# Rotary embedding on one core: the second batch's load is issued by SyncE instead of ScalarE

## The chip, the cores and the metric

The kernel runs on one core of a Trainium2 chip. The metric is the device time of one execution in microseconds (us); less is better. Three executions were timed before the change.

## What is computed

The reference rotates pairs of halves of each head (16 heads of 64 numbers) by tables that depend on the position in the sequence alone:

```python
# x: (16, 512, 1024) f32; cos, sin: (512, 32) f32
x = x.reshape(16, 512, 16, 64)
x1, x2 = x[..., :32], x[..., 32:]
out = concatenate([x1 * cos - x2 * sin, x1 * sin + x2 * cos], axis=-1)
```

So 33.55 MB are read, 33.55 MB are written, and three elementwise passes lie between: a product with cos, a product of the swapped halves with plus or minus sin, and a sum.

## The kernel before

**Tiles.** The work is cut into 64 "rows", each a block of 128 partitions x 1024 numbers (half a megabyte). Ten tiles of x hold them. Tiles 0, 1, 8 and 9 are one batch each (4 rows, 2 MB, moved in pieces of 16 KB); tiles 2 to 7 are two batches each (8 rows, 4 MB, moved in pieces of 32 KB). In the list `tiles`, tile 1 is batch 1, "the second batch". Rows are numbered u = 0 to 63 through all tiles, so tile 7 is rows 48 to 55, tile 8 rows 56 to 59 and tile 9 rows 60 to 63.

**Memory.** `x_sb` is a ring of 40 rows: tiles 0 to 5. Tiles 6 to 9 reuse its places, so their loads wait for stores of earlier tiles. Results are written in place, and stored from there.

**Engines.** For each row VectorE (DVE) multiplies x by cos into PSUM (`mul`, line 293). GpSimd (POOL) multiplies the swapped halves by sin into one of six buffers `t2_sb` (line 257); row 3 of each pair tile is done by VectorE instead (line 286). The sum is made in one of two ways: VectorE adds (`comb`, line 304), or, for the 21 rows with u mod 8 in 1, 3, 6 of the pair tiles and of rows 56 to 59, TensorE adds by a product with the identity (line 224) and ScalarE (ACT) copies the sum out of PSUM (line 191). PSUM has three places for rows (`t1_ps`), so `mul` of row u needs row u-3 to be gone.

**Tables.** cos and sin (64 KB each) are loaded into `stage` (line 174). VectorE copies cos for the single tiles (line 264), ScalarE makes the signed sin table (lines 182, 183), and TensorE and ScalarE make the pair tables (lines 208, 186, 187). GpSimd's first row waits for the sin table, VectorE's first row for the cos table.

**Transfers.** All loads are issued by ScalarE, from `load` (line 153), in this order: tile 0, cos, sin, tile 1, tiles 2 to 5. After row 17 ScalarE waits until the stores of tiles 0 and 1 have landed and loads tile 6; after row 25 it waits for the store of tile 2 and loads tile 7; after row 33 it waits for the store of tile 3 and loads tiles 8 and 9. ScalarE works in order, so its copy of the next row (line 191) stands behind that wait. Stores are issued by SyncE (SP), tile by tile (line 161), each when all rows up to the tile's last are summed. The last act is SyncE's wait for the stores (line 162). Loads and stores thus use two DMA queues: q10 for what ScalarE issues, q1 for what SyncE issues.

Of the kernel before, what the change touches and what calls it, by code (L numbers as in the profile page):

```python
# [6 lines left out]
def bass_split_heads_rope_kernel(  # L7
# [60 lines left out]
    with ExitStack() as stack:  # L68
# [44 lines left out]
        def in_dram(single, pairs, t):  # L113
            b, n = tiles[t]
            return single[b] if n == R1 else pairs[:, b:b + 2, :]

        def in_sbuf(t):
            b, n = tiles[t]
            k = b * R1 % RING
            return x_sb[:, k:k + n].rearrange("p n h t d -> p (n h t d)")  # L120

        def where(u):
            t, r = rows[u]
            return t, r, u % RING
# [7 lines left out]
        def wait_added(eng, u):  # L132

            if n_pe[u]:
                eng.wait_ge(sem_a, n_pe[u])
            if n_comb[u]:
                eng.wait_ge(sem_v, n_comb[u])
# [10 lines left out]
        def stores_of(k):  # L148

            return sum(b * R1 // R2 == k for b, _ in tiles)  # L150

        def load(eng, t):
            eng.dma_start(in_sbuf(t), in_dram(x1, x2, t)).then_inc(sem_in[t], 16)  # L153

        def on_sync(sp):
            for u in range(NU):
                t, r, k = where(u)
                if r == tiles[t][1] - 1:
                    wait_added(sp, u)
                    k = u // R2  # L160
                    sp.dma_start(in_dram(o1, o2, t), in_sbuf(t)).then_inc(sem_out[k] if k < EARLY else sem_rest, 16)
            sp.wait_ge(sem_rest, 16 * sum(stores_of(k) for k in range(EARLY, NU // R2)))

        def on_scalar(ae):
            later = {}
            for t, (b, n) in enumerate(tiles):
                if b * R1 + n <= RING:
                    load(ae, t)
                else:

                    later.setdefault((b * R1 - RING) // R2 * R2 + R2 - 1 + LAG, []).append(t)
                if t == 0:
                    for i, (table, sem) in enumerate(((cos, sem_cos), (sin, sem_sin))):
                        ae.dma_start(stage[:, i, :], table.rearrange("(s r) d -> s (r d)", r=R1)).then_inc(sem, 16)  # L174

            ae.wait_ge(sem_i, 2)
            ae.activation(  # L177
                pick[:], ident[:].rearrange("q (s k) -> q k s", k=2)[:, :, :, None].broadcast_to([P, 2, P // 2, 2]), COPY
            ).then_inc(sem_g, 1)
            ae.wait_ge(sem_sin, 16)  # L180
            sv = stage[:, 1, :].rearrange("s (r d) -> s r d", d=HALF)
            ae.activation(s1_sb[:, :, 0, :], sv, COPY, scale=-1.0)  # L182
            ae.activation(s1_sb[:, :, 1, :], sv, COPY).then_inc(sem_s, 1)  # L183
            ae.wait_ge(sem_t, 2)
            s2 = s2_sb[:].rearrange("p (k r) t d -> p k r t d", r=R1)
            ae.activation(s2[:, :, :, 0, :], pair_ps[:, :, 1, :, :], COPY, scale=-1.0)  # L186
            ae.activation(s2[:, :, :, 1, :], pair_ps[:, :, 1, :, :], COPY).then_inc(sem_s, 1)  # L187
            for u in range(NU):
                if PE2[u]:
                    ae.wait_ge(sem_e, n_pe[u])  # L190
                    ae.activation(xs[:, u % RING, :], t1_ps[:, u % NT1, :], COPY).then_inc(sem_a, 1)  # L191
                for t in later.get(u, ()):
                    k = (tiles[t][0] * R1 - RING) // R2
                    ae.wait_ge(sem_out[k], 16 * stores_of(k))
                    load(ae, t)
# [65 lines left out]
        def on_vector(ve):  # L261
# [49 lines left out]
            for u in range(NU + LEAD):  # L311
                if u < NU:
                    mul(u)
                if u >= LEAD and not PE2[u - LEAD]:
                    comb(u - LEAD)

        on_sync(nc.sync)
        on_scalar(nc.scalar)
        on_gpsimd(nc.gpsimd)
        on_tensor(nc.tensor)  # L320
# [34 lines left out]
```

## Time and profile before

| What | us |
| --- | --- |
| median of the three timed runs (161.17 to 161.33) | 161.23 |
| span of the profiled execution, first to last instruction | 160.3 |

The page gives no time of the profiled execution but its span; the 0.9 us by which the median is longer lie around the first and last instruction, and are taken as the same for any version. Below, 0 is the first instruction.

Busy in that span: GpSimd 134.9 us (84%), VectorE 130.3 us (81%), TensorE 72.8 us, ScalarE 24.4 us. The DMA engines moved 67.26 MB at a mean of 419 GB/s, and 0.99 of 16 engines' span is the two queues' share (49.6% and 48.9%).

The trace gives each transfer's issue and the time from issue to landing:

| Tile | load issued | load landed | store issued | store landed |
| --- | --- | --- | --- | --- |
| 0 | 0.81 | 8.8 | 20.48 | 39.1 |
| cos / sin | 1.21 / 1.69 | 9.0 / 9.2 | | |
| 1 | 2.17 | 14.1 | 31.02 | 53.6 |
| 2 | 2.87 | 23.8 | 47.50 | 73.6 |
| 3 | 3.47 | 38.4 | 63.68 | 93.06 |
| 4 | 4.13 | 52.9 | 81.07 | 112.1 |
| 5 | 4.79 | 72.3 | 102.73 | 126.7 |
| 6 | 53.60 | 91.9 | 119.57 | 141.2 |
| 7 | 73.60 | 111.3 | 135.58 | 150.7 |
| 8 | 93.08 | 126.5 | 143.57 | 155.5 |
| 9 | 93.45 | 141.0 | 151.70 | 160.3 |

A row of the profile's timeline reads: start, duration, engine, line, operation, output<-input, count of merged instructions, and in brackets the idle time before and what ended it. "ACTq" and "SPq" are the queues that ScalarE and SyncE issue transfers from; their rows are the issue, not the transfer.

### The profile page before, as it was taken

What the parts mean: (1) busy time and instruction counts of PE and PEld (TensorE: products, weight loads), DVE (VectorE), ACT (ScalarE), POOL (GpSimd) and SP (SyncE); (2) the same over time, 40 slices, a digit from 0 to 9 for tenths busy, and PEclk for the clock granted to TensorE, in tenths of its full rate; (3) what the DMA queues carried; (4) which work ended last, traced back from release to release, by engine and by line L of the source; (5) the groups of instructions that cost most, each with busy time, mean ns of one, the idle gap of its engine ahead of it and who ended that gap; (6) DMA issues with size and microseconds to landing.
All of it is one profiled execution on the core that took longest, in us unless ns stands there. A gap on an engine that the chain in (4) does not pass through costs nothing.

```text
span 160.3 us, 522 instructions
## 1 busy us (share of the span) xinstructions
PE 72.8 (45%) x94; PEld 24.0 (15%) x94; DVE 130.3 (81%) x117; ACT 24.4 (15%) x27; POOL 134.9 (84%) x64
## 2 busy tenths in 40 slices
PE   6050004478357936660847105489458435850000
PEld 1020002022202211210221002022202111220000
DVE  0069998599989999996999709899889999999500
ACT  0420000203120222022012010201220402040000
POOL 1059999999999999999999999699999999289400
PEclk9955555557755587689687965555555977699555
DMA  5999999999999999999999999999999999999896
GB/s 147 409 441 474 409 450 409 425 429 429 446 429 458 417 411 466 409 433 401 450 433 425 425 409 458 409 433 433 411 429 462 441 417 401 450 441 441 376 450 294
DMA packets 3170, 67.26 MB, mean 419 GB/s; under 512 B 352, under 2 KB 608, under 8 KB 608
## 3 DMA queue, kind: packets, MB, share of 16 engines
q10 hardware_dynamic: 1728, 33.69, 49.6%
q1 hardware_dynamic: 1440, 33.56, 48.9%
q14 instruction: 2, 0.02, 0.0%
HBM read 33.69 MB, written 33.55 MB: 419 GB/s over the span
## 4 chain that ended last, share of the span: by engine, by line
DMA 60%; POOL 13%; DVE 8%; PE 7%; issue 3%; ACT 2%; ACTq 1%; DVEq 0%
DMA x_sb<-in_x_dram 41%; DMA out_dram<-x_sb 18%; POOL t_sb L257 13%; PE t_ps L224 7%; DVE t_ps L293 5%; DVE x_sb L304 3%; ACT x_sb L191 2%; ACTq L153 1%; ACTq L174 1%; DVE t_sb L286 0%; DVEq L303 0%
## 5 line engine op out<-in xcount | busy, mean ns | idle before, releaser
L257 POOL TENSOR_TENSOR t_sb<-x_sb,s_sb 128x1024 f32<-128x1024 f32 x58 | 134.2, 2346 | 14.8 <-ACT s_sb L183 8.5
L224 PE MATMUL t_ps<-t_sb,ident 128*128 128x512 f32 x84 | 68.0, 957 | 63.0 <-DVE t_ps L293 39.2
L293 DVE TENSOR_TENSOR t_ps<-x_sb,pair_ps 128x1024 f32<-128x1024 f32 x48 | 57.7, 1223 | 9.9 <-ACT x_sb L191 9.8
L304 DVE TENSOR_TENSOR x_sb<-t_ps,t_sb 128x1024 f32<-128x1024 f32 x43 | 52.4, 1218 | 2.6 <-POOL t_sb L257 2.6
L224 PEld LDWEIGHTS t_ps<-t_sb,ident 128*128 128x128 f32 x84 | 22.1, 290 | 108.9 <-DVE t_ps L293 74.6
L191 ACT ACTIVATE x_sb<-t_ps 128x1024 f32<-128x1024 f32 x21 | 21.5, 1023 | 109.9 <-PE t_ps L224 96.9
L293 DVE TENSOR_TENSOR t_ps<-x_sb,tab_ps 128x1024 f32<-128x1024 f32 x16 | 19.3, 1222 | 0.1
L286 DVE TENSOR_TENSOR t_sb<-x_sb,tab_ps 128x1024 f32<-128x1024 f32 x6 | 7.3, 1213 | 0.0
L264 DVE COPY tab_ps<-stage 128x128 f32<-128x128 f32 x1 | 0.3, 294 | 7.8 <-DMA stage<-in_cos_dram 7.8
L208 PE MATMUL pair_ps<-stage,pick 128*128 128x256 f32 x4 | 2.0, 667 | 5.4 <-DMA stage<-in_sin_dram 5.4
L201 PE MATMUL t_ps<-zero 128*128 128x512 bf16 x6 | 2.7, 627 | 1.3 <-DVE zero L262 1.3
L208 PEld LDWEIGHTS pair_ps<-stage,pick 128*128 128x128 f32 x4 | 1.2, 324 | 6.4 <-issue 6.3
L177 ACT ACT_TABLE_LOAD x1 | 1.3, 1283 | 5.5 <-issue 5.5
L201 PEld LDWEIGHTS t_ps<-zero 128*128 128x128 bf16 x6 | 0.7, 136 | 2.4 <-DVE zero L262 1.2
L262 DVE MEMSET zero<- 128x256 uint32 x1 | 0.3, 272 | 0.9 <-PEq L337 0.9
L186 ACT ACTIVATE s_sb<-pair_ps 128x256 f32<-128x256 f32 x1 | 0.4, 383 | 1.7 <-PE pair_ps L208 1.7
L182 ACT ACTIVATE s_sb<-stage 128x128 f32<-128x128 f32 x1 | 0.3, 309 | 2.1 <-DMA stage<-in_sin_dram 2.1
L235 POOL MEMSET ident<- 128x128 f32 x1 | 0.2, 204 | 0.3 <-POOLq L337 0.3
L177 ACT ACTIVATE pick<-ident 128x256 f32<-128x256 f32 x1 | 0.4, 416 | 0.0
L187 ACT ACTIVATE s_sb<-pair_ps 128x256 f32<-128x256 f32 x1 | 0.4, 379 | 0.0
L237 POOL TENSOR_SCALAR_AFFINE_SELECT ident<-ident 128x128 f32<-128x128 f32 x1 | 0.3, 292 | 0.1
L337 POOL MEMSET const-float32-0.0<- 128x1 f32 x1 | 0.1, 98 | 0.3 <-issue 0.3
(6 smaller groups left out, 1.0 us busy)
## 6 DMA issues: line engine op xcount, KB each, us to landing
x_sb<-in_x_dram ACTq DMA_DIRECT2D x6, 4096.0 KB, 38.0
out_dram<-x_sb SPq DMA_DIRECT2D x6, 4096.0 KB, 25.0
x_sb<-in_x_dram ACTq DMA_DIRECT2D x4, 2048.0 KB, 22.6
out_dram<-x_sb SPq DMA_DIRECT2D x4, 2048.0 KB, 15.2
stage<-in_cos_dram ACTq DMA_DIRECT2D x1, 64.0 KB, 7.8
stage<-in_sin_dram ACTq DMA_DIRECT2D x1, 64.0 KB, 7.5
```

What stands on the lines that cost most here:

```text
L153: eng.dma_start(in_sbuf(t), in_dram(x1, x2, t)).then_inc(sem_in[t], 16)
L174: ae.dma_start(stage[:, i, :], table.rearrange("(s r) d -> s (r d)", r=R1)).then_inc(sem, 16)
L177: ae.activation(pick[:], ident[:].rearrange("q (s k) -> q k s", k=2)[:, :, :, None].broadcast_to([P, 2, P // 2, 2]), COPY).then_inc(sem_g, 1)
L186: ae.activation(s2[:, :, :, 0, :], pair_ps[:, :, 1, :, :], COPY, scale=-1.0)
L191: ae.activation(xs[:, u % RING, :], t1_ps[:, u % NT1, :], COPY).then_inc(sem_a, 1)
L201: pe.matmul(t1_ps[:, k, b * BANK:(b + 1) * BANK], zero[:, 0:P], zero[:], start=True, stop=True).then_inc(sem_w, 1)
L208: pe.matmul(pair_ps[:, k].rearrange("p c r d -> p (c r d)"), pick[:, k].rearrange("q s b -> q (s b)"), stage[:].rearrange("q c f -> q (c f)"),
L224: ins = pe.matmul(t1_ps[:, u % NT1, b * BANK:(b + 1) * BANK], ident[:], t2[:, b * BANK:(b + 1) * BANK], start=False, stop=True, skip_group ...
L257: pl.tensor_tensor(t2_sb[:, u % NT2, :, :, :], swapped(k), over_heads(s_of(t, r)), mult).then_inc(sem_p, 1)
L286: ve.tensor_tensor(t2_sb[:, u % NT2, :, :, :], swapped(k), over_heads(v_ps), mult)
L293: ve.tensor_tensor(t1_ps[:, u % NT1, :].rearrange("p (h d) -> p h d", d=HALF), x_sb[:, k, :, :, :].rearrange("p h t d -> p (h t) d"), c_of ...
L304: ve.tensor_tensor(xs[:, k, :], t1_ps[:, u % NT1, :], t2_sb[:, u % NT2, :, :, :].rearrange("p h t d -> p (h t d)"), add,).then_inc(sem_v, 1)
```

## The change

SyncE issues the load of tile 1 as its first act, before its first store. ScalarE skips tile 1 in its loop and goes from the sin table straight to tile 2. Buffer, semaphore, size and pieces of the load are the same; what changes is which queue carries it and when it is issued. No wait is added or removed.

```diff
         def on_sync(sp):
+            load(sp, 1)
             for u in range(NU):
                 t, r, k = where(u)
                 if r == tiles[t][1] - 1:
...
             for t, (b, n) in enumerate(tiles):
+                if t == 1:
+                    continue
                 if b * R1 + n <= RING:
                     load(ae, t)
```

## The prediction

> **What bounds the kernel now.** I read the page first, for the share of the DMA engines:
>
> ```profile
> span 160.3 us, 522 instructions
> ...
> DMA  5999999999999999999999999999999999999896
> GB/s 147 409 441 474 409 450 409 425 429 429 446 429 458 417 411 466 409 433 401 450 433 425 425 409 458 409 433 433 411 429 462 441 417 401 450 441 441 376 450 294
> ```
>
> After the first slice the engines that move data never rest. No byte is added or removed, so the end stays where it is as long as some queue always holds work; the question is whether a hole opens. For that I need the start, the sharing between the queues, and the end. The start, from the timeline:
>
> ```profile
> 0.81 0.37 ACTq L153 DMA_DIRECT2D x_sb<-in_x_dram  x1
> ...
> 1.21 0.46 ACTq L174 DMA_DIRECT2D stage<-in_cos_dram  x1
> ...
> 1.69 0.45 ACTq L174 DMA_DIRECT2D stage<-in_sin_dram  x1
> ...
> 2.17 3.27 ACTq L153 DMA_DIRECT2D x_sb<-in_x_dram  x5
> ...
> 9.04 0.29 DVE L264 COPY tab_ps<-stage 128x128 f32<-128x128 f32 x1 [7.84 <-DMA stage<-in_cos_dram]
> 9.26 0.31 ACT L182 ACTIVATE s_sb<-stage 128x128 f32<-128x128 f32 x1 [2.08 <-DMA stage<-in_sin_dram]
> ...
> 9.85 32.35 POOL L257 TENSOR_TENSOR t_sb<-x_sb,s_sb 128x1024 f32<-128x1024 f32 x14 [8.48 <-ACT s_sb L183]
> ```
>
> All computing waits for tile 0, cos and sin, which are alone at the head of the queue and land at 8.8, 9.0 and 9.2; GpSimd starts at 9.85 and pauses little after. How two busy queues share, from the DMA view of two stretches: 26 to 52 us, where stores go in 16 KB pieces against loads in 32 KB pieces,
>
> ```profile
> q10 hardware_dynamic: 251, 7.34, 65.9%
> q1 hardware_dynamic: 254, 3.85, 34.6%
> ```
>
> and 56 to 72 us, where both have 32 KB pieces (columns: packets, MB, share of the engines):
>
> ```profile
> q1 hardware_dynamic: 114, 3.47, 50.9%
> q10 hardware_dynamic: 120, 3.41, 49.3%
> ```
>
> The queues take turns piece by piece: equal counts, bytes by size. The middle, from the timeline at 92 to 98 us:
>
> ```profile
> 93.08 2.40 ACTq L153 DMA_DIRECT2D x_sb<-in_x_dram  x2
> 95.52 1.02 ACT L191 ACTIVATE x_sb<-t_ps 128x1024 f32<-128x1024 f32 x1 [8.86 <-issue]
> 96.58 1.23 DVE L293 TENSOR_TENSOR t_ps<-x_sb,pair_ps 128x1024 f32<-128x1024 f32 x1 [5.31 <-ACT x_sb L191]
> ```
>
> ScalarE stands until tile 3's store lands (93.06), issues two loads in 2.40 us, and only then empties a place of PSUM that VectorE has wanted for 5.31 us. From there VectorE hardly pauses (three gaps of 0.41 us), so its later times hang on that landing. The end:
>
> ```profile
> 135.58 16.46 SPq L161 DMA_DIRECT2D out_dram<-x_sb  x3
> ...
> 141.02 9.27 POOL L257 TENSOR_TENSOR t_sb<-x_sb,s_sb 128x1024 f32<-128x1024 f32 x4 [3.92 <-DMA x_sb<-in_x_dram]
> ...
> 148.10 1.23 DVE L304 TENSOR_TENSOR x_sb<-t_ps,t_sb 128x1024 f32<-128x1024 f32 x1
> 150.40 1.23 DVE L304 TENSOR_TENSOR x_sb<-t_ps,t_sb 128x1024 f32<-128x1024 f32 x1 [1.08 <-POOL t_sb L257]
> ```
>
> The store of tile 7 is issued at 135.58, 5.6 us before tile 6's lands (141.2); tile 9's at 151.70, 3.8 us before tile 8's lands (155.5). These leads keep the engines full at the end. After 141 us there are no loads left to fill a hole.
>
> **Step 1: the issue.** ScalarE loses one issue (about 0.6 us; five take 3.27 us), so tiles 2 to 5 are issued that much earlier, into a queue that is full until they come: worth 0. ScalarE's next work waits for sin anyway. SyncE gains one issue; its next duty is the first store at 20.48, so nothing stands behind it: 0. A rule speaks against a gain: the Trainium skill, "DMA: Bandwidth & Descriptors", section "Issuing engines are not separate DMA queues", says that issuing from several engines saves only the time to issue; taken alone it would leave 161.2 us, while the turns above make it worse than that.
>
> **Step 2: the start.** Tile 0 now shares the engines with tile 1, 16 KB pieces against 16 KB pieces, from the first. Before, 2 MB cost 4.85 us (tile 1 landed 14.05, sin 9.25, 4.80 apart). Tile 0 ends after 15 or 16 turns instead of 8, and cos and sin stand behind it in its queue. The bytes of the four transfers are the same, so sin, now the last of them, lands where tile 1 did: 14.05, a shift of 4.8. If tile 0 leads by a turn, cos and sin end one piece earlier: 4.2 (4.85/8 = 0.6 a piece). With no sharing it would be 0, which the rows above speak against. I take 4.8. GpSimd starts at 14.65, and its fourth row, which makes the first store, shifts alike: 20.48 becomes 25.3.
>
> **Step 3: the middle.** Stores now enter the queue 4.8 us later. Their rate is set by turns against a load queue that is still full, so each lands 4.8 later: tiles 0 and 1 at 58.4, tile 2 at 78.4, tile 3 at 97.9. Loads use the freed turns and run about 4.8 us ahead: tile 5 at 67.5, tile 6 at 87.1, tile 7 at 106.5. Is the load queue ever empty? Tile 6 is issued at 58.4 (before 67.5), tile 7 at 78.4 (before 87.1), tiles 8 and 9 from 97.9 (before 106.5): no. So no hole here, and nothing lost yet. But ScalarE's stand also ends 4.8 later, and VectorE's stall of 5.31 with it: computing gets nothing back. GpSimd's waits for loads (3.92 and 0.38 us) vanish, but VectorE, which trails GpSimd by some 6 us at tile 7 (row 55: GpSimd ends at 127.9, VectorE's sum starts at 134.3), has none of them to gain.
>
> **Step 4: the end.** Tile 7's store is issued at 135.58 + 4.8 = 140.4. Up to 141.2 all other bytes are the same, so tile 6's store still lands at 141.2: the lead shrinks from 5.6 to 0.8. How long a transfer into idle engines takes to start bounds the hole. From below: tile 9's store landed 4.85 after tile 8's, with no start to pay. From above: tile 0's load, alone in a cold queue, took
>
> ```profile
> DMA to landing us min/median/max: 8.0/8.0/8.0
> ```
>
> from issue to landing for the same 2 MB, so 8.0 - 4.85 = 3.15 of start. I take 2.35, nearer to the load, since that row contains its very first pieces. Tile 7 then lands at 140.4 + 2.35 + 9.7 = 152.4 (before 150.7), tile 8 at 157.3, tile 9 at 162.1, if tile 9's store comes in time. It comes so: VectorE's last tile loses its wait of 1.08 on GpSimd, which now has its data early, so its last sum shifts by 4.8 - 1.17 (150.40 would be 149.23 behind the sum that starts at 148.10): issue at 151.70 + 3.63 = 155.3. Alone it lands 4.85 + 2.35 = 7.2 later: 162.5, with the bounds 160.2 and 163.3. The later of the two counts: 162.5 instead of 160.3, that is +2.2, on the median 163.4. A page's price for one transfer (same page, section on the anatomy of one DMA, fitted for GpSimd's transfers: 2.0 us and bytes at 436 GB/s) gives an estimate of 6.8 instead of the row's 8.0, and 163.0 instead of 163.4 for the sum.
>
> The unknowns: the shift (4.2 to 4.8: -0.6), the start (3.15: +0.8; none at all: -2.3, which would leave only the absorbed case below), TensorE's clock, which is granted by turns at 0.5 and 1.0 and makes the three gaps of 0.41 (up to -1.2, or as much more), and the 2.40 us of two issues at 93.08, where two issues at the start take 0.8 (up to -1.6). Not all fall on one side: +0.6 to +3.2.
>
> **The rivals.** *Absorbed, 161.2.* The engines stay full and the bytes alone set the end. It holds if tile 7's store shifts by less than about 3 us (its lead of 5.6 less 2.35) and tile 9's issue by less than about 1.5 (3.8 less 2.35), or two or three of the unknowns fall together: 4.8 - 1.6 - 1.2 = 2.0 at tile 7, 0.8 at tile 9. For it: the DMA row full of nines, GpSimd's 4.3 us of waits for loads. Against it: VectorE, not GpSimd, releases tile 7, and waits for no load. *No sharing, 161.2 or a little less.* SyncE's pieces come only after tile 0, cos and sin; then the start is as before, and perhaps the ramp (the first 4 us carry 147 GB/s) is a little fuller, by at most 0.5 us. The equal piece counts speak against it. *Whole shift, 164.6 to 166.0.* The last tile does not catch up its 1.17, or a stall of ScalarE grows: 156.5 + 7.2 = 163.7 of span for the first, 160.3 + 4.8 for the rest of the shift.
>
> **How the numbers follow.** A hole at the end as summed: 0.77. Whole shift: 0.10. Absorbed: 0.09, a fifth of it with a small loss. No sharing: 0.04, mostly a little faster. A measurement of this kernel can tell about 0.2% (0.3 us) from no change: faster 0.03, same 0.08, slower 0.89. The range 161.8 to 164.6 takes in the first case and the near edge of the third.
>
> **What would show it.** Sin landing near 14 us, GpSimd starting near 14.6 and the first store near 25; the waits for loads on GpSimd gone; tile 3's store landing near 97.9 and VectorE starting again near 101.4; the DMA row with a dent at about 141 to 143 us; last store issued near 155.3. I am wrong if GpSimd starts before 13 us, if tile 7's store is issued before 138.5, or if the DMA row has no dent and the end still moves.

## The result, and the profile after

The changed kernel takes 162.03 us (median of eight, 161.41 to 163.18) where the kernel before takes 161.26 (eight, 161.17 to 161.49): ratio 1.0045, 95% interval 1.0027 to 1.0064, some 0.7 us slower. Forecast were 2.2 us. The mechanism is the one that was summed; its size was three times too large. The profiled execution of the changed kernel has a span of 160.9 us and a time of 162.30, so 1.4 us lie around the span.

The page:

```profile
span 160.9 us, 522 instructions
...
DMA  5999999999999999999999999999999999999997
GB/s 183 424 428 432 497 416 391 391 411 428 452 424 448 399 436 458 448 399 440 464 399 432 473 399 407 497 395 395 456 454 432 440 407 420 391 391 391 428 420 326
...
POOL 32%; DMA 26%; PE 14%; DVE 12%; issue 6%; ACT 4%; ACTq 1%; DVEq 0%
```

The DMA row has no visible dent, which by its letter is one of the prediction's signs of being wrong. But a slice is 4 us, and the hole that opened is 1 us (slices 35 to 37 have 391 GB/s, the whole span 418); the windows at the end of this section show it. The chain of work that ended last (last line) tells more: before, 60% of it was DMA; now DMA has 26%, and the computing engines have most of the rest. The start, from the timeline (the changed kernel's lines are 3 higher than before's, so L267 is L264, L296 is L293, L260 is L257, L194 is L191):

```profile
0.80 0.38 SPq L153 DMA_DIRECT2D x_sb<-in_x_dram  x1
0.81 0.40 ACTq L153 DMA_DIRECT2D x_sb<-in_x_dram  x1
...
13.60 0.29 DVE L267 COPY tab_ps<-stage 128x128 f32<-128x128 f32 x1 [12.40 <-DMA stage<-in_cos_dram]
13.78 0.31 ACT L185 ACTIVATE s_sb<-stage 128x128 f32<-128x128 f32 x1 [7.22 <-DMA stage<-in_sin_dram]
...
14.37 2.35 POOL L260 TENSOR_TENSOR t_sb<-x_sb,s_sb 128x1024 f32<-128x1024 f32 x1 [13.00 <-ACT s_sb L186]
```

Tile 0 lands at 13.4, tile 1 at 13.2, cos at 13.6, sin at 13.8: the four transfers end together, as turns piece by piece make them. GpSimd starts 4.5 us later than before. The middle, at 97 to 101 us:

```profile
98.06 0.86 ACTq L153 DMA_DIRECT2D x_sb<-in_x_dram  x2
98.97 1.02 ACT L194 ACTIVATE x_sb<-t_ps 128x1024 f32<-128x1024 f32 x1 [7.54 <-DMA out_dram<-x_sb]
100.03 1.23 DVE L296 TENSOR_TENSOR t_ps<-x_sb,pair_ps 128x1024 f32<-128x1024 f32 x1 [3.24 <-ACT x_sb L194]
```

Tile 3's store lands at 98.04 (97.9 was forecast), but the two load issues behind it take 0.86 us instead of 2.40, and VectorE goes on at 100.03, not at 101.4. The end, with the time of tile 9's store from issue to landing in the second fence:

```profile
139.36 15.48 SPq L162 DMA_DIRECT2D out_dram<-x_sb  x3
...
152.09 2.35 DVE L307 TENSOR_TENSOR x_sb<-t_ps,t_sb 128x1024 f32<-128x1024 f32 x2
```

```profile
L162 SPq DMA_DIRECT2D out_dram<-x_sb x1: 338/338/338, 154.5 to 154.5; - x1
DMA to landing us min/median/max: 6.3/6.3/6.3
```

VectorE ends without its wait on GpSimd, as forecast. Tile 7's store is issued at 139.36, 1.04 us before tile 6's lands (140.40), and lands at 150.89. That is 10.49 after tile 6's, where a second profile of the kernel before has 9.49: the hole, 1.0 us. Tiles 8 and 9 follow after 4.92 and 5.04 instead of 4.84 and 4.82. The windows from 136 to 144 us show the hole too (the last two columns: share of the DMA engines, GB/s), first the second profile of before, then the changed kernel:

```profile
136.00:144.00 8.00, 5.76 (x8) 1.87 (x6) 6.91 (x7) 2.05 (x2) 4.37 (x3) 0.68 1.03 442
```

```profile
136.00:144.00 8.00, 5.62 (x7) 1.51 (x5) 7.59 (x8) 1.02 (x1) 8.00 (x4) 0.52 0.80 344
```

The packets in the trace give it piece by piece. In the changed kernel the 16 engines are through with tile 6's store between 139.3 and 140.0, up to 1.1 us before its landing is signalled at 140.40, and tile 7's first piece starts at 140.56, 1.20 us after its issue. On average an engine stands idle 1.06 us between 136 and 144 us, and 0.01 us in the second profile of before.

### The profile page after: what moved, and what is told of

Its sections match the earlier page's. It is cut to its first block, busy times and chain, and to the rows that moved or that the text cites. A ratio compares the mean times of both kernels' runs of the same rounds, so it can differ in the third digit from the quotient of the medians.

```text
span 160.9 us, 522 instructions
## 1 busy us (share of the span) xinstructions
PE 73.0 (45%) x94; PEld 23.5 (15%) x94; DVE 130.1 (81%) x117; ACT 24.4 (15%) x27; POOL 134.8 (84%) x64
## 4 chain that ended last, share of the span: by engine, by line
POOL 32%; DMA 26%; PE 14%; DVE 12%; issue 6%; ACT 4%; ACTq 1%; DVEq 0%
POOL t_sb L260 32%; DMA out_dram<-x_sb 19%; PE t_ps L227 14%; DMA stage<-in_sin_dram 7%; DVE t_ps L296 6%; DVE x_sb L307 4%; ACT x_sb L194 4%; ACTq L153 1%; DVE t_sb L289 1%; ACTq L177 0%; ACT s_sb L185 0%; ACT s_sb L186 0%; DVEq L293 0%
## 5 line engine op out<-in xcount | busy, mean ns | idle before, releaser
L260 POOL TENSOR_TENSOR t_sb<-x_sb,s_sb 128x1024 f32<-128x1024 f32 x58 | 134.1, 2356 | 13.7 <-ACT s_sb L186 13.0
L296 DVE TENSOR_TENSOR t_ps<-x_sb,pair_ps 128x1024 f32<-128x1024 f32 x48 | 57.7, 1222 | 8.9 <-ACT x_sb L194 8.9
L194 ACT ACTIVATE x_sb<-t_ps 128x1024 f32<-128x1024 f32 x21 | 21.5, 1024 | 109.0 <-PE t_ps L227 96.9
L227 PEld LDWEIGHTS t_ps<-t_sb,ident 128*128 128x128 f32 x84 | 21.6, 284 | 108.4 <-DVE t_ps L296 68.9
L296 DVE TENSOR_TENSOR t_ps<-x_sb,tab_ps 128x1024 f32<-128x1024 f32 x16 | 19.3, 1222 | 0.6 <-ACT x_sb L194 0.6
L267 DVE COPY tab_ps<-stage 128x128 f32<-128x128 f32 x1 | 0.3, 295 | 12.4 <-DMA stage<-in_cos_dram 12.4
```

The lines of the kernel that those rows point to most:

```text
L227: ins = pe.matmul(t1_ps[:, u % NT1, b * BANK:(b + 1) * BANK], ident[:], t2[:, b * BANK:(b + 1) * BANK], start=False, stop=True, skip_group ...
L260: pl.tensor_tensor(t2_sb[:, u % NT2, :, :, :], swapped(k), over_heads(s_of(t, r)), mult).then_inc(sem_p, 1)
L296: ve.tensor_tensor(t1_ps[:, u % NT1, :].rearrange("p (h d) -> p h d", d=HALF), x_sb[:, k, :, :, :].rearrange("p h t d -> p (h t) d"), c_of ...
```

## The experiments

**The theory**: tile 1's pieces push tile 0 and the tables back; all stores shift with them; ScalarE's wait for tile 3's store passes the shift on to VectorE; tile 7's store comes too late to keep the engines full. **Its rivals**: a second queue of loads is slow by itself; or the loss is in proportion to the delay, wherever it is made. All ratios are against the kernel before on the same chip, with their 95% intervals.

**The changed kernel again, and the same delay on one queue.** No edit in the first. In the second, tile 1 stays on ScalarE, and the tables go behind it:

```diff
-                if t == 0:
+                if t == 1:
                     for i, (table, sem) in enumerate(((cos, sem_cos), (sin, sem_sin))):
```

> The changed kernel once more, as the reference for this group and a second profile of it. Theory 'late start, hole at the end': GpSimd starts at 14.4, the stores of tiles 0 to 3 land 5 us later than before, the DMA row has a dent near 139 to 141 us, and the time is 161.4 to 163.2 us, scattered more widely than before because the end now hangs on VectorE and ScalarE, not on the bytes. Where the second of the two load issues after tile 3's store takes 2.0 us instead of 0.5, the time should be about 1.5 us longer. Rival 'two queues of loads are slower': no dent, and the share of the DMA engines in 8 to 24 us below 1.0.

> All loads on ScalarE's queue as before the change, but cos and sin behind tile 1: one queue, the start late by 4.8 us, nothing on SyncE. Theory 'late start': GpSimd starts at 14.6, tile 7's store is issued 3.3 to 4.8 us later than before (138.9 to 140.4), the hole is there, and the time is 162.0 to 163.2 us. As the ramp of the first 4 us is that of one queue, tile 6's store lands at 141.2, not 140.4, and the time is a little above that of the changed kernel. Rival 'two queues of loads are slower' expects 161.2 us, since there is one queue.

The changed kernel: 161.86 us, ratio 1.0042 (1.0019 to 1.0065), last landing 160.40. One queue: 161.70, 1.0031 (1.0006 to 1.0056), GpSimd starting at 14.63, tile 7's store at 138.63, last landing 160.24. Nothing is issued by SyncE at the start there, and the loss is the same within the intervals: it is the delay that costs. Nor does the changed kernel's second profile show the rival's sign, less busy DMA engines at 8 to 24 us: their share there is 1.04, and 1.01 in the second profile of before. Three numbers of the expectation for one queue failed: it was no slower than the changed kernel, its time lay under the 162.0 forecast, and tile 7's store was issued before 138.9.

**Half the delay**, one queue: the tables behind the first two rows of tile 1, the other two after them. (`half(eng, t, i)` loads share i of two equal shares of tile t's rows. Its definition, and the waits for such a tile, raised from 16 to 32, are not shown here and below.)

```diff
+                if t == 1:
+                    half(ae, 1, 1)      # rows 2 and 3
...
                 if t == 0:
+                    half(ae, 1, 0)      # rows 0 and 1
```

> One queue, half the delay: cos and sin behind the first two rows of tile 1 (all 128 partitions, 8 KB pieces), the other two rows after them. The start is late by 2.4 us (GpSimd at 12.2). Theory 'late start, hole at the end': tile 7's store is issued at 136.5 to 138.0, still early enough; no dent, time as before (161.4 to 161.6 us). A loss in proportion to the delay expects half of what the two late versions lost (0.3 to 0.4%), that is about 161.8 us.

161.42 us, ratio 1.0003 (0.9995 to 1.0012). GpSimd starts at 12.05, 2.4 late; tile 7's store is issued at 135.92, 4.9 us before tile 6's lands. The first 2.4 us cost nothing that can be measured; a loss in proportion, 0.15 to 0.2%, lies just above the interval.

**Twice the delay**, one queue: the tables behind tile 1 and four rows of tile 2.

```diff
+                if t == 2:
+                    half(ae, 2, 1)
...
-                if t == 0:
+                if t == 1:
+                    half(ae, 2, 0)
```

> One queue, about twice the delay: cos and sin behind tile 1 and the first four rows of tile 2, so the start is late by 9.65 us (GpSimd near 19.3). Theory 'late start, hole at the end': once the lead is used up, every further microsecond counts in full. Against the changed kernel (late by 4.5) everything shifts by another 5: tile 7's store issued near 144.2, tile 9's near 159.3, last landing 6.3 us later at 165.5 to 166, against 159.8 to 160.3 before; ratio 1.033 to 1.038. A loss in proportion to the delay, drawn through the changed kernel's 0.4% at 4.5 us, expects 0.9%.

162.91 us, ratio 1.0106 (1.0089 to 1.0122). GpSimd starts at 19.50, but the rest of the theory's numbers failed: I had taken every microsecond beyond the lead to count in full, and 5 us more cost 1. The loss in proportion, 0.9%, came nearest here; what speaks against it is half the delay, and below the later wait, with the whole delay and no loss. What gave way is VectorE's stall, from its waits:

```profile
DVE t_ps L303 <- ACT x_sb L201: 4.9, 9, 1.4
```

(total, times, longest), against 9.5 and 3.2 in the changed kernel. All early loads have landed at 62.63, tile 6's is issued only at 62.84, and its first piece moves at 67.10, 4.3 us later. The DMA view of 62.7 to 67 us has packets of the store queue q1 and none of q10 (the share passes 100% because a packet counts whole where it starts):

```profile
q1 hardware_dynamic: 61, 2.00, 117.4%
```

Meanwhile the stores have all the turns: tile 2's store takes 16.2 us after tile 1's instead of 20, and tile 3's lands at 98.37, no later than in the changed kernel. ScalarE hardly stands. Now GpSimd is the path:

```profile
POOL 71%; DMA 10%; issue 7%; DVE 3%; PE 2%; ACTq 1%; ACT 1%
```

It runs without a pause from 19.50 to 153.53. Holes open all the same at the end: an engine stands idle 0.97 us on average between 136 and 158 us. That the chain passes a delay on in full holds only as long as the load queue has work.

**Finer stores at the end**, in the changed kernel and in the one before: tiles 7, 8 and 9 are stored in two halves of rows each.

```diff
-                if r == tiles[t][1] - 1:
+                n = tiles[t][1]
+                if t in (7, 8, 9) and (r + 1) % (n // 2) == 0:
...
+                    sp.dma_start(d[:, f] if n == R1 else d[:, :, f], in_sbuf(t)[:, f]).then_inc(sem_rest, 16)
+                elif r == n - 1:
```

> The changed kernel with the stores of tiles 7, 8 and 9 issued in two halves of rows each, so that data is at hand earlier at the end. Theory 'late start, hole at the end': the first half of tile 7's store is issued near 131 us, before tile 6's store has landed, so the dent in the DMA row at 138 to 141 goes; the last half tile is issued near 154 and needs about 4 us, so it no longer sets the end; span 159.6 to 160.0, time 161.0 to 161.3 us on a chip where the kernel before takes 161.5, with less scatter. Rival 'the loss is made at the start, by sharing': 161.9 us as without the finer stores.

> The same finer stores in the kernel before, where tile 7's store already waits in the queue. Theory: no hole to close, 161.4 to 161.6 us, the same as before. If finer stores are a gain by themselves (an earlier last landing), it is faster by as much as the changed kernel is with them, some 0.6 us.

Changed kernel: 161.54 us, ratio 1.0016 (1.0006 to 1.0025). Before: 161.36, 1.0003 (0.9994 to 1.0012). The first half of tile 7 is issued at 132.80, no idle time of the DMA engines is left between 136 and 158 us, and the loss falls from 0.42 or 0.45% to 0.16% (the intervals of 0.42 and 0.16 still overlap); where there was no hole, finer stores bring nothing. The rest was larger than I expected, hence the next pair.

**ScalarE's waits three rows later** (all three of them), in both kernels, leaves the late start and takes VectorE's stall away:

```diff
-    LAG = 10
+    LAG = 13
```

> The changed kernel with ScalarE's wait for a store (and the load behind it) three rows later: after rows 20, 28 and 36 instead of 17, 25 and 33. In the changed kernel ScalarE stands until 98.0 us with row 35's sum not copied, and VectorE is idle 3.2 us for it (1.9 at the stand before). If the loss goes through this stand, VectorE's idle there shrinks to under 1.5 us at the later one, tile 7's store is issued at 136 to 138 instead of 139, the dent at 138 to 142 goes, tile 9's store is issued near 152, and the time is that of the kernel before (ratio 0.999 to 1.001) with little scatter, though the start is as late as ever. If the loss is made at the start or by the load pieces that stretch when the first stores begin (26 to 34 us), the ratio stays at 1.002 to 1.005.

> The same later wait in the kernel before, as the control. There VectorE idles longer at the stand (4.6 to 5.3 us), but tile 7's store waits in the queue anyway and the bytes set the end: ratio 0.999 to 1.001. If VectorE's stall costs time here too, it is faster, by up to 0.5%.

Changed kernel: 161.36 us, ratio 0.9999 (0.9984 to 1.0013). Before: 161.44, 0.9999 (0.9980 to 1.0018). The changed kernel's timeline with the later wait:

```profile
98.75 1.22 DVE L307 TENSOR_TENSOR x_sb<-t_ps,t_sb 128x1024 f32<-128x1024 f32 x1
100.38 1.23 DVE L296 TENSOR_TENSOR t_ps<-x_sb,pair_ps 128x1024 f32<-128x1024 f32 x1 [0.41 <-ACT x_sb L194]
```

Tile 3's store lands at 98.05, in the changed kernel at 98.04, but VectorE is three rows further by then (this is row 41, not row 38) and stands 0.41 us instead of 3.24. VectorE's waits for ScalarE's copies sum to 3.8 us instead of 9.5. Tile 7's store is issued at 132.39, even before the 136 to 138 expected and 8.1 us before tile 6's lands, and the last landing is 159.87, where the second profile of before has 159.78. The start is late by 4.5 us as ever. So the loss goes through ScalarE's stands; with them gone, the late start is free. In the control VectorE's stall at this stand falls as well, from the 4.56 of the second profile of before:

```profile
95.99 1.23 DVE L293 TENSOR_TENSOR t_ps<-x_sb,pair_ps 128x1024 f32<-128x1024 f32 x1 [0.50 <-ACT x_sb L191]
```

Tile 7's store is issued there at 130.29 instead of 133.93, and nothing is gained. Neither version beats the kernel before: there the bytes set the end, and no edit of these touches them.

**Two queues without a delay.** Two attempts to have the second queue but not the late start. First half a tile each, cut by partitions (tile 0, or tile 1, in two halves of 64 partitions, the first issued by SyncE):

```diff
+        def half(eng, t, i):
+            h = slice(i * P // 2, (i + 1) * P // 2)
+            eng.dma_start(in_sbuf(t)[h], in_dram(x1, x2, t)[h]).then_inc(sem_in[t], 16)
...
+            half(sp, 0, 0)      # in on_sync; half(sp, 1, 0) for tile 1
...
+                    half(ae, 0, 1)      # in on_scalar, in the tile's old place
```

> Tile 0 is loaded in two halves of 64 partitions, one from SyncE and one from ScalarE at the same time; tile 1 stays on ScalarE in its old place. No delay of the start, but two queues in the ramp. Theory of the fuller ramp: tile 0 and the tables land at 8.3 to 8.8, all later landings 0.4 to 0.5 us earlier, no hole, time 160.7 to 160.9 us. If the ramp's gain belongs to something else, 161.2 us. Rival 'two queues of loads are slower': above 161.2 us.

> SyncE loads only the first 64 partitions of tile 1 at the start, ScalarE the other 64 in the old place. Half the dose: start late by about 2.2 us (GpSimd at 12.0). Theory 'late start': tile 7's store is issued 1 to 2.4 us later (136.6 to 138.0), still ahead of tile 6's landing by more than it needs to start, so no hole; and the fuller ramp with two queues (279 GB/s against 180 between 2 and 3 us) brings every landing forward by 0.5: time 160.7 to 160.9 us, faster than before. Without the gain of the ramp 161.2. Rival 'two queues of loads are slower' expects half the loss, 161.6 us; a loss in proportion to the delay expects the same.

Both expectations failed by far: tile 0 halved took 165.62 us, ratio 1.0264 (1.0240 to 1.0288), tile 1 halved 170.79, 1.0580 (1.0553 to 1.0607). The DMA view of tile 0 halved, 4 to 10 us, shows why:

```profile
DMA packets 90, 1.47 MB, mean 246 GB/s; under 512 B 0, under 2 KB 0, under 8 KB 0
```

The engines are busy throughout and move 246 GB/s: the 16 KB pieces of this stretch take 1.13 to 1.15 us instead of 0.61. Cut by rows instead, two rows of all 128 partitions in each half:

```diff
-            h = slice(i * P // 2, (i + 1) * P // 2)
+            h = slice(i * e, (i + 1) * e)      # e: numbers of two rows; taken of the second axis
```

> Tile 0 in two halves of two rows each over all 128 partitions (8 KB pieces), one from SyncE and one from ScalarE. Of the earlier split by partitions the trace showed each 16 KB piece taking 0.94 to 1.14 us instead of 0.61 while only 64 partitions were written by a transfer. If that was what cost 4 us, this split costs nothing: tile 0 lands at 8.4 to 8.8, GpSimd starts at 9.4 to 9.8, ratio 0.997 to 1.000. If splitting tile 0 over two queues is what costs, it is again near 1.026.

161.40 us, ratio 1.0007 (0.9991 to 1.0024), tile 0 landing at 8.9, and in the same stretch of the DMA view

```profile
DMA packets 564, 2.57 MB, mean 429 GB/s; under 512 B 64, under 2 KB 320, under 8 KB 320
```

So a transfer cut to 64 partitions is slow, and a tile spread over two queues is not. Why the cut costs twice as much in tile 1 as in tile 0 was not looked into. The two halved kernels say nothing on the change itself. That the second queue fills the ramp better by itself, as I took from the changed kernel's first 3 us, is not borne out: here tile 2 lands at 23.7, as with one queue.

**The tables alone from SyncE**, and no longer from ScalarE, everything else as before:

```diff
         def on_sync(sp):
+            for i, (table, sem) in enumerate(((cos, sem_cos), (sin, sem_sin))):
+                sp.dma_start(stage[:, i, :], table.rearrange("(s r) d -> s (r d)", r=R1)).then_inc(sem, 16)
```

> The kernel before, but SyncE issues cos and sin as its first act, beside ScalarE's load of tile 0; tile 1 stays on ScalarE. Two queues in the ramp, and almost no bytes in the way of tile 0. Theory: tile 0 lands as before or up to 0.4 us later (8.6 to 9.2), the tables long before it, GpSimd starts at 8.9 to 9.6, no hole; the end hangs on the bytes and gains at most the fuller ramp, 0 to 0.4 us: ratio 0.997 to 1.000. If a second queue of loads at the start costs by itself, it is above 1.001.

161.46 us, ratio 1.0019 (1.0002 to 1.0036), and a surprise in the timeline:

```profile
7.19 0.29 DVE L263 COPY tab_ps<-stage 128x128 f32<-128x128 f32 x1 [5.99 <-DMA stage<-in_cos_dram]
9.21 2.36 DVE L292 TENSOR_TENSOR t_ps<-x_sb,tab_ps 128x1024 f32<-128x1024 f32 x2 [1.73 <-DMA x_sb<-in_x_dram]
12.30 0.31 ACT L181 ACTIVATE s_sb<-stage 128x128 f32<-128x128 f32 x1 [6.23 <-DMA stage<-in_sin_dram]
```

cos, 64 KB in pieces of 512 bytes, lands at 7.16, and sin at 12.28, after tile 0 (9.1) and though it has nothing but cos ahead of it in its queue. A table has as many pieces for an engine as a 2 MB tile (8), and each waits for one piece of the other queue: 8 turns of 0.61 us are 4.9. The start, expected at 8.9 to 9.6, is at 12.90, 3.3 us later than in the second profile of before. The ratio above 1.001 is what a second queue that costs by itself would give; but tile 0 in halves of rows had a second queue of loads at the start, no delay and no loss. The Trainium skill ("DMA: Bandwidth & Descriptors", section "Queues, rings and completion order") says that an engine goes round its queues packet by packet, and that a packet has typically 9 to 17 descriptors; the turns agree, but here each 512-byte row had a turn of its own.

**The kernel before, once more**, for a second profile:

> The kernel before, for a second profile. In the first one the second of the two load issues at 93.08 us took 2.02 us; in the four profiles since, 0.49 to 0.51. If 2.02 was one execution's accident, it takes 0.5 here, VectorE starts again near 95 instead of 96.6, and the span is near 160.1, as no step at the end depends on it. If it belongs to this kernel, it is 2.0 again.

Last landing 159.78 us, span 159.8, time 161.23, so 1.4 us lie around this span too; the two issues:

```profile
92.23 1.69 ACTq L153 DMA_DIRECT2D x_sb<-in_x_dram  x2
93.97 1.02 ACT L191 ACTIVATE x_sb<-t_ps 128x1024 f32<-128x1024 f32 x1 [9.45 <-issue]
```

The long issue is there again (the second of the two takes 1.32 us). In all five profiles in which GpSimd starts before 10 us it takes 1.3 to 2.0 us, in all ten with a later start 0.47 to 0.51. So it is no accident of one execution. In the first group the previous load had landed less than 2 us before this issue; but so it had with tile 0 halved by partitions (1.4 us before), and there it took 0.49. The cause stays open.

The versions side by side, from one profiled execution each, so that the last landings scatter by some tenths (half the delay's is the slowest of its eleven runs) and the ratio is the better measure of the time (us; "lead" is from tile 7's store's issue to tile 6's landing, for the finer stores of its first half):

| Version | GpSimd starts | VectorE's stall at the stand | lead | tile 9's store issued | last landing | ratio |
| --- | --- | --- | --- | --- | --- | --- |
| before, second profile | 9.60 | 4.56 | 6.7 | 151.18 | 159.78 | 1 |
| tile 1 on SyncE (the change) | 14.37 | 3.24 | 1.0 | 154.51 | 160.85 | 1.0045 |
| the same, again | 14.29 | 3.32 | 1.5 | 154.04 | 160.40 | 1.0042 |
| tables behind tile 1 | 14.63 | 3.50 | 2.1 | 153.91 | 160.24 | 1.0031 |
| tables on SyncE | 12.90 | 3.49 | 2.7 | 153.07 | 159.90 | 1.0019 |
| half the delay | 12.05 | 3.62 | 4.9 | 151.00 | 160.21 | 1.0003 |
| twice the delay | 19.50 | 0.67 | 3.1 | 155.10 | 161.44 | 1.0106 |
| the change, finer stores | 14.22 | 3.46 | 7.8 | 153.91 | 160.15 | 1.0016 |
| the change, wait 3 rows later | 14.19 | 0.41 | 8.1 | 149.61 | 159.87 | 0.9999 |

By the packets, the mean idle time of a DMA engine between 136 and 144 us follows the lead: 1.06 us at a lead of 1.0, 0.58 at 1.5, 0.27 at 2.1, 0.01 or less at 2.7 and above. Only twice the delay has 0.29 at 3.1; there the engines end tile 6's store over 2.2 us (139.44 to 141.69), in the changed kernel over 0.7.

## Why the prediction was off

The path was right, and two terms of its sum were too large: the wait behind the pair of load issues at ScalarE's stand, taken as unchanged at 2.40 us where it measured 0.86 (step 3), and the start of the last store, taken as 2.35 us where it measured 1.5 (step 4). The start of tile 0's load and of the computing (step 2) and the landings of the middle came as forecast.

**Step 1, the issue: right.** Both are issued at 0.80 and 0.81, and ScalarE's earlier end of issuing (4.8 instead of 5.4) bought nothing. The Trainium skill's rule ("DMA: Bandwidth & Descriptors", section "Issuing engines are not separate DMA queues"), that issuing from several engines saves only the time to issue, agrees with that. The same section says that the transfers of all engines interleave; here that is what cost, as tile 0 landed at 13.4 instead of 8.8.

**Step 2, the start: right, a little large.** 4.5 us instead of 4.8.

**Step 3, the middle: right in kind.** Stores of tiles 0 and 1, 2 and 3 landed at 58.76, 78.69 and 98.04 (forecast 58.4, 78.4, 97.9), loads 5, 6 and 7 at 67.3, 86.6 and 106.0 (67.5, 87.1, 106.5); GpSimd's waits for loads are gone. That ScalarE's stand passes the delay on to VectorE was shown by the later wait, which removes the loss. But "VectorE's stall ends 4.8 later" failed: it ended 3.5 later (100.03 for 96.58), because the pair of issues takes 0.86 us in the changed kernel and took 2.40 before (1.69 in the second profile). I had listed this as an unknown worth up to 1.6 us and kept it in the sum at zero.

**Step 4, the end: the hole is there, its price was mis-sized.** The start of a transfer into idle engines was the other term that failed. I took 2.35 us between bounds of 0 and 3.15, nearer to tile 0's load. Tile 9's store of 2 MB took 6.35 us from issue to landing in the changed kernel, 6.36 in its repetition, 6.33 and 6.34 in two other late versions (tables behind tile 1, twice the delay): 1.5 us over the 4.85 of its bytes. It was not wholly alone, as I had assumed: it was issued 1.30 us before tile 8's store landed, and its first piece moved at 155.37, 0.86 us after the issue and just behind tile 8's last. The load in the cold queue was no good measure of a store into a running one. The Trainium skill's price for one transfer (same page, section "Anatomy of one DMA — SWDGE (gpsimd) path", fitted for GpSimd's transfers) gives an estimate of 6.8, between the two.

Put together, tile 9's store was to be issued at 155.3 and land 7.2 later, at 162.5; it was issued at 154.5 and landed 6.35 later, at 160.85. Of the 1.65 us too many, 0.8 lie in the issue (the pair of issues, less what four gaps of 0.41 instead of three, and smaller ones, gave back) and 0.85 in the landing.

**The profiled execution of before** was itself longer than most: a span of 160.3 with 1.4 us around it is 161.7, while the runs shown had a median of 161.23. I put 0.9 around it and took its landings as the typical ones. The second profile has all of the end 0.5 us earlier. Against that one the changed kernel's last landing is 1.07 us later, against the first 0.55; the medians lie 0.77 apart. The forecast took both of its ends, 160.3 and 162.5, from the first profile, so its 2.2 us don't hang on this.

**The rivals.** *Absorbed* was nearer than its chance of 0.09 says: its condition, a lead longer than the start of a transfer, was of the right kind. The lead has to be longer than the 1.5 us of a start, though, since the engines run dry up to 1.1 us before the landing to which it is counted: at 1.5 and 2.1 us there still was idle time. *Whole shift* and *no sharing* did not come.

**What scattered.** The changed kernel's 20 executions spread over 1.8 us, the kernel before's first eight over 0.3, and the 23 and 29 of it beside the first two groups of experiments over 1.3 and 0.7. In the 20 runs of the changed kernel, the five with a granted clock below 0.66 took 161.54 to 163.22 (median 163.14), the other fifteen 161.41 to 162.56 (median 161.85). In those 52 runs of the kernel before, four had such a clock and took 161.14 to 161.59, no more than the rest; in the 34 runs of half the delay, finer stores and the later wait, four had such a clock, with a median of 161.5 beside 161.4. That fits an end that hangs on TensorE's sums, ScalarE's copies and VectorE's gaps rather than on bytes; no experiment took the clock alone.

**Still open**: with finer stores 0.16% was left without a hole. Adding up the pieces in the trace, those of the loads run 0.65 us over their usual time for each engine at 24 to 36 us in the changed kernel, when the first stores join, and 0.2 in the second profile of before. The later wait has the same excess (0.76) and no loss, so it is not enough by itself.

## What to carry to other kernels

A load issued on a second queue is not put behind the first queue's: in all four pairs of piece sizes seen here it took every other turn, so what is needed first came later. In a kernel whose bytes set the end, a late start is free as long as every store at the end is issued well before the previous one lands (2.7 us was enough here in the versions with the usual spread of the engines, 2.1 was not) and no computing engine becomes the path, as GpSimd did at twice the delay. Read that lead from the profile, and for each engine in between ask what wait passes the delay on. And when one term has bounds as far apart as the whole effect, the effect is known only in sign.

## What the runs showed of the hardware

- Two queues take turns by pieces, not bytes: a 64 KB table in 512-byte pieces took 5.1 us beside 16 KB pieces (cos at 7.16, sin at 12.28), 0.2 us behind a tile in the same queue.
- A transfer's first piece moves 1.0 to 1.2 us after its issue where the engines are idle (tile 0's load before, issued at 0.81: 1.82; tile 7's store in the changed kernel, issued at 139.36: 140.56). Where its own queue is empty and the other keeps the engines busy, it takes 3.4 to 4.3 us (first store before, issued at 20.48: 23.90; in the changed kernel, issued at 25.00: 28.60; tile 6's load at twice the delay, issued at 62.84: 67.10).
- A load cut into two of 64 partitions each is slow: 16 KB pieces at 1.13 to 1.15 us, 246 GB/s, where the same tile cut by rows, over 128 partitions, ran at 429. The Trainium skill ("DMA: Bandwidth & Descriptors", section "Rules for kernel authors") advises one 128-partition transfer since two halves serialize; that speaks of no gain, and here it was a loss of 2.6 and 5.8%.
- Two loads issued back to back by ScalarE in the middle of the kernel take 0.8 to 0.9 us in the versions with a late start and 1.7 to 2.4 us in those without; the cause was not found.
